# Tiles 3 and 7 by quarters in the second column half of the second products, their parts kept in idle buffers, two sums merged

## Chip, cores and metric

The kernel runs on one core of a Trainium2 chip. The metric is device time in microseconds: the median of three runs of the whole program. TensorE (PE) multiplies matrices, VectorE (DVE) and ScalarE (ACT) work element by element, GpSimd (POOL) does a few small steps, and SyncE (SP) issues most transfers. Each engine works through its own queue in order, and waits for the others by semaphores.

## The reference

A decoder layer over 512 tokens of 1024 columns: a SwiGLU feed-forward layer (FFN 1), a token mixer, and a second SwiGLU layer (FFN 2), all in float32, each between two RMS norms.

```python
def swiglu_ffn(x, w_in, w_out):
    gate, up = jnp.split(x @ w_in, 2, axis=-1)
    return (jax.nn.silu(gate) * up) @ w_out
...
x = x + 0.5 * rms_norm(swiglu_ffn(rms_norm(x, norm_pre[l, 0]), ffn1_w_in[l], ffn1_w_out[l]),
                       norm_post[l, 0])
mixed = token_mixer(rms_norm(x, norm_pre[l, 1]), w_mix_in[l], ...)
x = x + rms_norm(mixed, norm_post[l, 1])
x = x + 0.5 * rms_norm(swiglu_ffn(rms_norm(x, norm_pre[l, 2]), ffn2_w_in[l], ffn2_w_out[l]),
                       norm_post[l, 2])
```

D_MODEL is 1024, D_FF 2816, DEPTH 1. The change is in the second product of both feed-forward layers: h (512 x 2816) times w_out (2816 x 1024).

## The kernel before

Every float32 operand is kept as two parts, a rounded high part (a cast on ACT, line 273 for weights, 812 for h) and the remainder as a low part (a subtraction on DVE, line 275 for weights, 813 for h). A product of two such operands takes three matmuls: high by high, high by low, low by high.

`ffn_out` computes the second product. The 1024 output columns are done in two halves of 512. The 2816 rows of `w_out` are cut into 11 tiles of 256 rows; a tile's weights in one half are 256 x 512, held as 128 x 1024. `OUT[half]` gives the order of the tiles. Each tile is done in one of two ways:

- plain (line 893): 16 blocks of 128 x 128 by 256 columns, three matmuls each, 48 in all. DVE makes one low part of the weights (128 x 1024), and one of h, unless the tile's h is kept from the first half (`AGAIN`, tiles 9 and 10).
- by quarters (line 901), for the tiles in `QUARTERED[half]`: the Strassen-Winograd form with seven products of quarters instead of eight, 42 matmuls. It wants sums of quarters of the weights (`sum_quarters`, four operations 128 x 256 on DVE, line 306) and of h (`h_sums`, on DVE, line 844). Its weights come as two sets: first the low part of three quarters as loaded (128 x 768), then, once the sums stand and ACT has cast them, the low part of the four summed quarters (128 x 1024, the variable `v` in `quartered`). Between the last sum on DVE and the low part of `v` on DVE lies a cast on ACT.

The low and high parts of three quarters of h, the tile's "parts" (`h_quarters`), last from the first half to the second where both go by quarters, in places of the buffers of the transposed input (`x_place`, table `PLACES`; tiles 2, 4, 6, 8). Tiles 3 and 7, by quarters in the first half only, have their parts in two buffers of the "raw" ring for that time, and their sums in the scratch tile `hsum`. The summed h that `quartered` multiplies is split anew in each half, into a ring of three buffers (`s_place`).

`more` runs two or three tiles ahead of the products, so the order of the splits on ACT and DVE follows from `OUT`, `QUARTERED` and the depth of the rings. Weights are loaded into a ring of five buffers (raw2), and their split parts lie in four places (`WBUF`). A load is issued by SP when its buffer comes free; SP's queue is in order, and a load whose buffer isn't free holds what is behind it.

The last four tiles of the second half (`LAST = 4`) are done chunk by chunk: `chunk(i)` computes group i of 128 tokens over all four tiles, after which `post1` norms it and adds it to x, and after FFN 1 the mixer's norm, transposes and first products (`head`) follow. The common sums of the products by quarters (`common`, `add`, line 863) are added before chunk 0 is complete. In the first half of `ffn_out` all eleven tiles go through one after the other, and `post0` takes the half's result (y, line 475) from the PSUM banks while the second half begins.

Of the kernel before, what the change touches and what calls it, by code (L numbers as in the profile page):

```python
# [9 lines left out]
F32R = mybir.dt.float32r  # L10
AF = mybir.ActivationFunctionType
ALU = mybir.AluOpType
PSUM = bass.MemoryType.PSUM

P = 128
T = 512
D = 1024
# [5 lines left out]
RAW, WBUF, PAD, LATE, NEXT, FRONT, STEP = 3, 4, 128, 112, 64, 96, 16  # L23
PAIRS = NF // 2
# [54 lines left out]

QUARTERED = [(2, 3, 4, 6, 7, 8), (2, 4, 6, 8)]
OUT = [list(range(PAIRS)), [9, 2, 4, 10, 6, 8, 0, 1, 3, 5, 7]]
LAST = 4
PLACES, LATER = {2: 1, 4: 2, 6: 0, 8: 3}, {0: (1, 0), 7: (2, 3)}

AGAIN, ROWS = (9, 10), (18, 19, 20, 21)

# [27 lines left out]
class Layer:  # L116
# [705 lines left out]
    def h_quarters(self, k2, n=None):  # L822

        src = self.by_chunk(k2)
        parts = self.x_place(n) if n is not None else [
            self.wp.tile([P, D], F32R, tag="raw", bufs=RAW, name=self.nm("once"))[:, P - 2 * STEP :] for _ in range(2)
        ]
        parts = [v[:, : 3 * QUARTER].rearrange("p (k c t) -> p k c t", c=2, t=P) for v in parts]
        self.two_parts(*(v[:, 0] for v in parts), src[:, 0, 1])
        self.two_parts(*(v[:, 1:] for v in parts), src[:, 1])  # L830
        return [[None] + [v[:, j] for j in range(3)] for v in parts]
# [5 lines left out]
    def h_sums(self, k2, stay):  # L837

        a = self.by_chunk(k2)
        f = self.hf[:, 2 * k2 : 2 * k2 + 2, :]  # L840
        if not stay:
            f = self.sp.tile([P, 2, T], F32, tag="xn", bufs=1, name=self.nm("hsum"))
        v = f.rearrange("p k (c u t) -> p k u c t", u=2, t=P)
        tt = lambda out, x, y, op: self.nc.vector.tensor_tensor(out, x, y, op=op)
        tt(v[:, 0, 0], a[:, 0, 1], a[:, 0, 0], ALU.subtract)
        tt(v[:, 1, 0], v[:, 0, 0], a[:, 1, 0], ALU.add)
        for k in range(2):
            tt(v[:, k, 1], a[:, k, 1], v[:, 1, 0], ALU.subtract)
        return f

    def s_tile(self, f):
# [6 lines left out]
    def ffn_out(self, gpost_row, scale, after, trans, head):  # L858
# [4 lines left out]
        tt = lambda out, a, b, op: nc.vector.tensor_tensor(out, a, b, op=op)  # L863
        seq = [(half, k2) for half in range(2) for k2 in OUT[half]]
        made = deque((h, None) for h in self.hs)
# [3 lines left out]
        def more(n):  # L869
            while count[0] < min(n, len(seq)):  # L870
                half, k2 = seq[count[0]]
                count[0] += 1
                if k2 in QUARTERED[half]:
                    if k2 not in kept:
                        stay = k2 in QUARTERED[1]
                        kept[k2] = self.h_quarters(k2, PLACES.get(k2)), self.h_sums(k2, stay)
                    a, f = kept[k2]
                    made.append((a, self.s_tile(f)))
                elif half and k2 in AGAIN:
                    made.append(again.popleft())  # L880
                else:
                    made.append((self.h_tile(k2, self.x_place(*LATER[k2]) if half and k2 in LATER else None), None))
                    if not half and k2 in AGAIN:
                        again.append(made[-1])
# [47 lines left out]
        def add(C, T, u):  # L932
            for v in range(2):
                tt(C[u][v], C[u][v], T[u, v], ALU.add)
# [9 lines left out]
        for half in range(2):  # L944
            C = [[self.ps() for _ in range(2)] for _ in range(2)]
            M, T, left = None, None, len(QUARTERED[half])
            for m, k2 in enumerate(OUT[half][: PAIRS - LAST * half]):
                more(n + 2)
# [9 lines left out]
                else:  # L958
                    w = self.pull()
                    more(len(seq) if half and m == PAIRS - LAST - 1 else n + 3)  # L960
                    for i in (0, 2, 1, 3):
# [13 lines left out]
        ws = []  # L975
        for k2 in OUT[1][-LAST:]:
            ws.append(self.pull())
            more(n + 1)
            n += 1
        hs = [made.popleft()[0] for _ in range(LAST)]  # L980

        add(C, T, 1)

        def chunk(i):
            vn = [(v, n) for v in range(2) for n in range(LAST)]
            if i == 0:

                vn.sort(key=lambda f: f[1])
            for v, n in vn:
                plain(C, ws[n], hs[n], i, v, False)  # L990
                if v and i == NT - 1:
                    self.drop(ws[n])
                if v and n == LAST - 1 and i == 0:
                    add(C, T, 0)
                if n == LAST - 1:
                    yield 2 - v
# [78 lines left out]
    def ffn_items(self, name, w_in, w_out):  # L1075
# [47 lines left out]
        for h in range(2):  # L1123
            for k2 in OUT[h]:
                src = w_out[k2 * 2 * P : (k2 + 1) * 2 * P, h * 512 : (h + 1) * 512].rearrange("(k p) d -> p k d", p=P)
                key = (name, "out", h, k2)
                made.append(Item(key, [Load(key, src, 2, 512, "raw2", 5, 8)], sums=k2 in QUARTERED[h]))
                if k2 in QUARTERED[h]:
                    made.append(Item(key, ()))
# [688 lines left out]
```

## Time and profile before

| | |
|---|---|
| median of 3 runs | 937.53 us (937.38 to 937.99) |
| profiled execution | 939.23 us, span of the trace 937.5 us |
| PE busy | 929.0 us (99% of the span), 7471 matmuls and transposes |
| DVE busy | 772.9 us (82%) |
| ACT busy | 511.5 us (55%) |
| POOL busy | 107.1 us (11%) |

The second product of FFN 1 begins at about 224 us of the span and its last matmuls start at 340.79 us, with the mixer's first norm and transposes between them; that of FFN 2 begins at about 816 us and runs to the end. In rows of the timeline the columns are the start and the time until the last of the joined instructions ends (us), the engine, the line, the operation, what it writes and reads, shape and count; in brackets how long the engine stood idle before it and what released it. L275 is line 275.

### The profile page before, as it was taken

Reading aid. Unit: us, or ns where it says so; the run is one execution under the profiler, and the core shown is the slowest. Engines: PE = TensorE matmul, PEld = TensorE weight load, DVE = VectorE, ACT = ScalarE, POOL = GpSimd, SP = SyncE. Lnnn points to the kernel's source line nnn. Section 1 sums busy time; section 2 is a strip of 40 time slices with the busy share of each in tenths; the row PEclk is TensorE's granted clock in tenths of the full one; section 3 lists DMA queues with packets and bytes.
Section 4 is the critical chain, followed back from the end, with each engine's and each line's share of the span. In section 5 each row is a group of like instructions: output and inputs, shape, how many; then the busy total and the mean of one; then the engine's idle time right before and its main releaser. Section 6 shows DMA issues by size and latency. Waiting matters only on the chain.

```text
span 937.5 us, 18056 instructions
## 1 busy us (share of the span) xinstructions
PE 929.0 (99%) x7471; PEld 894.4 (95%) x7471; DVE 772.9 (82%) x1044; ACT 511.5 (55%) x735; POOL 107.1 (11%) x172
## 2 busy tenths in 40 slices
PE   9999999999999999999999999999999999999997
PEld 7999999999999999998887887899999999999997
DVE  6899988889988876698846665799899889998884
ACT  7645455557456467956632445595354545655541
POOL 3530000000001045200011310314000000000101
PEclk9999999999999999999999999999999999999999
DMA  9252443332352034421312124352354435324212
GB/s 317 89 157 91 128 126 108 99 108 78 116 164 91 24 87 121 111 68 45 91 45 68 46 91 143 104 181 67 115 158 135 136 116 157 108 90 131 78 45 91
DMA packets 86956, 101.35 MB, mean 108 GB/s; under 512 B 4277, under 2 KB 66777, under 8 KB 86874
## 3 DMA queue, kind: packets, MB, share of 16 engines
q1 hardware_dynamic: 86586, 99.68, 34.8%
q8 instruction: 58, 0.95, 0.4%
q10 hardware_dynamic: 288, 0.52, 0.2%
q14 instruction: 24, 0.20, 0.1%
HBM read 98.10 MB, written 2.10 MB: 107 GB/s over the span
## 4 chain that ended last, share of the span: by engine, by line
PE 61%; ACT 1%; DMA 0%; DVE 0%; issue 0%; POOL 0%; DVEq 0%; POOLq 0%; ACTq 0%; SPq 0%
PE ps L603 22%; PE ps L893 7%; PE ps L533 6%; PE ps L901 5%; PE ps L179 5%; PE ps L181 4%; PE ps L180 4%; PE ps L1307 2%; PE ps L348 1%; PE ps L543 1%; PE ps L1482 0%; DMA raw<-in_ffn_w_in_dram 0%; PE ps L1393 0%; PE ps L1589 0%; PE ps L1562 0%; PE ps L1348 0%
## 5 line engine op out<-in xcount | busy, mean ns | idle before, releaser
L273 ACT CAST w<-raw 128x1024 fp32r<-128x1024 f32 (+1 forms) x238 | 244.4, 1034 | 233.1 <-PE ps L603 93.5
L275 DVE TENSOR_TENSOR w<-raw,w 128x1024 fp32r<-128x1024 f32 (+1 forms) x238 | 291.6, 1232 | 36.1 <-ACT w L273 35.3
L603 PE MATMUL ps<-xq,w 128*128 128x256 f32 x2016 | 237.4, 277 | 0.0
L603 PEld LDWEIGHTS ps<-xq,w 128*128 128x128 f32 x2016 | 233.2, 188 | 0.0
L603 PE MATMUL ps<-sq,w 128*128 128x256 f32 x1512 | 178.3, 277 | 0.3
L603 PEld LDWEIGHTS ps<-sq,w 128*128 128x128 f32 x1512 | 174.6, 188 | 0.9 <-ACT ps L654 0.9
L893 PE MATMUL ps<-w,hs 128*128 128x256 f32 x960 | 113.0, 276 | 0.0
L893 PEld LDWEIGHTS ps<-w,hs 128*128 128x128 f32 x960 | 110.7, 188 | 0.0
L289 DVE TENSOR_TENSOR raw<-raw,raw 128x1024 f32<-128x1024 f32 x72 | 89.9, 1251 | 8.1 <-DMA raw<-in_ffn_w_in_dram 6.6
L179 PE MATMUL ps<-w,xq 128*128 128x512 f32 x192 | 78.8, 411 | 0.1
L180 PE MATMUL ps<-w,xq 128*128 128x512 f32 x192 | 74.9, 391 | 0.1
L181 PE MATMUL ps<-w,xq 128*128 128x512 f32 x192 | 75.0, 392 | 0.0
L438 POOL TENSOR_SCALAR col<-col 128x1 f32<-128x1 f32 x24 | 9.0, 377 | 513.8 <-ACT junk L437 513.7
L533 PE MATMUL ps<-xq,w 128*128 128x256 f32 x480 | 58.1, 282 | 0.0
L901 PE MATMUL ps<-w,hs 128*128 128x256 f32 x480 | 57.7, 276 | 0.0
L533 PEld LDWEIGHTS ps<-xq,w 128*128 128x128 f32 x480 | 56.9, 189 | 0.5 <-issue 0.5
L901 PEld LDWEIGHTS ps<-w,hs 128*128 128x128 f32 x480 | 55.9, 188 | 0.0
L179 PEld LDWEIGHTS ps<-w,xq 128*128 128x128 f32 x192 | 36.1, 188 | 8.3 <-issue 0.9
L181 PEld LDWEIGHTS ps<-w,xq 128*128 128x128 f32 x192 | 36.0, 188 | 8.2 <-DVE xq L355 0.3
L812 ACT CAST hs<-hf 128x1024 fp32r<-128x1024 f32 x32 | 33.7, 1052 | 17.4 <-PE ps L901 10.7
L180 PEld LDWEIGHTS ps<-w,xq 128*128 128x128 f32 x192 | 36.2, 188 | 7.2 <-DVE w L281 0.5
L813 DVE TENSOR_TENSOR hs<-hf,hs 128x1024 fp32r<-128x1024 f32 x32 | 39.1, 1221 | 1.3 <-ACT hs L812 1.2
(258 smaller groups left out, 1140.4 us busy)
## 6 DMA issues: line engine op xcount, KB each, us to landing
raw<-in_ffn_w_in_dram SPq DMA_DIRECT2D x98, 512.0 KB, 3.7
raw<-in_ffn_w_out_dram SPq DMA_DIRECT2D x44, 512.0 KB, 4.2
raw<-in_w_mix_in_dram SPq DMA_DIRECT2D x28, 512.0 KB, 3.7
raw<-in_w_mix_out_dram SPq DMA_DIRECT2D x8, 512.0 KB, 3.9
out_dram<-xs SPq DMA_DIRECT2D x8, 256.0 KB, 2.0
xs<-in_x_dram SPq DMA_DIRECT2D x6, 256.0 KB, 4.1
gpost<-in_norm_post_dram SPq DMA_DIRECT2D x3, 512.0 KB, 3.5
gpre<-in_norm_pre_dram SPq DMA_DIRECT2D x2, 512.0 KB, 4.5
```

Of the source, the lines that this page charges most:

```text
L179: mm(ps, sh, mh, start=start, stop=False, **kw)
L180: mm(ps, sh, ml, start=False, stop=False, **kw)
L181: mm(ps, sl, mh, start=False, stop=stop, **kw)
L273: nc.scalar.copy(hi, raw)
L275: self.low = nc.vector.tensor_tensor(lo, raw, hi.bitcast(F32), op=ALU.subtract)
L289: (nc.vector if late else nc.gpsimd).tensor_tensor(o, o, c, op=ALU.add)
L533: mm(ps[:, u0:u1], w[:, a, k, :], self.xop(k, b, u0, u1), start=k + n + m == 0, stop=k == ND - 1 and n == 2, skip_group_check=True,)
L603: self.nc.tensor.matmul(ps[:, c], wb[b][:, k, v], left[d][:, k, :], start=first and a + n + k == 0, stop=n == 2 and k == KH - 1, skip_grou ...
L812: self.nc.scalar.copy(hi, src)
L813: self.nc.vector.tensor_tensor(lo, src, hi.bitcast(F32), op=ALU.subtract)
L893: mm(out, a[kk][:, i * P : (i + 1) * P], w[:, b, kk, QUARTER * v : QUARTER * (v + 1)], start=begin and c == kk == n == 0, stop=kk == 1 and ...
L901: mm(ps[:, QUARTER * c : QUARTER * (c + 1)], A[a][:, c], B[b], start=begin and c == n == 0, stop=n == 2, skip_group_check=True,)
```

## The change

Tiles 3 and 7 go by quarters in the second half too, so both halves have the same six. Their parts now have to last into the second half: those of tile 3 stay in two buffers of "raw", those of tile 7 (`APART`) in one buffer of "raw" and in the tile of the norm's gain (`gpre`), which is not in use then. The sums of both stay in place in h (the `stay` branch of `h_sums`; the scratch `hsum` is no longer used). The second half's order is new, tile 10 moves from the fourth to the eighth place, and `LATER` names a place for tile 5's h alone. In `h_sums` two subtractions of 128 x 256 that share an operand become one of 128 x 512. The program has 7240 matmuls in its queue instead of 7264.

```diff
--- before.py
+++ after.py
@@ -79,10 +79,10 @@
 
 
 
-QUARTERED = [(2, 3, 4, 6, 7, 8), (2, 4, 6, 8)]
-OUT = [list(range(PAIRS)), [9, 2, 4, 10, 6, 8, 0, 1, 3, 5, 7]]
-LAST = 4
-PLACES, LATER = {2: 1, 4: 2, 6: 0, 8: 3}, {0: (1, 0), 7: (2, 3)}
+QUARTERED = [(2, 3, 4, 6, 7, 8), (2, 3, 4, 6, 7, 8)]
+OUT = [list(range(PAIRS)), [9, 2, 4, 3, 6, 8, 7, 10, 0, 1, 5]]
+LAST, APART = 4, 7
+PLACES, LATER = {2: 1, 4: 2, 6: 0, 8: 3}, {5: (2, 3)}
 
 AGAIN, ROWS = (9, 10), (18, 19, 20, 21)
 
@@ -822,9 +822,12 @@
     def h_quarters(self, k2, n=None):
 
         src = self.by_chunk(k2)
-        parts = self.x_place(n) if n is not None else [
-            self.wp.tile([P, D], F32R, tag="raw", bufs=RAW, name=self.nm("once"))[:, P - 2 * STEP :] for _ in range(2)
-        ]
+        once = lambda pool, tag, bufs, o: pool.tile([P, D], F32R, tag=tag, bufs=bufs, name=self.nm("once"))[:, o:]
+        if n is not None:
+            parts = self.x_place(n)
+        else:
+            places = [(self.wp, "raw", RAW, P - 2 * STEP), (self.cp, "gpre", 1, STEP // 2)]
+            parts = [once(*places[k2 == APART and m]) for m in range(2)]
         parts = [v[:, : 3 * QUARTER].rearrange("p (k c t) -> p k c t", c=2, t=P) for v in parts]
         self.two_parts(*(v[:, 0] for v in parts), src[:, 0, 1])
         self.two_parts(*(v[:, 1:] for v in parts), src[:, 1])
@@ -844,8 +847,7 @@
         tt = lambda out, x, y, op: self.nc.vector.tensor_tensor(out, x, y, op=op)
         tt(v[:, 0, 0], a[:, 0, 1], a[:, 0, 0], ALU.subtract)
         tt(v[:, 1, 0], v[:, 0, 0], a[:, 1, 0], ALU.add)
-        for k in range(2):
-            tt(v[:, k, 1], a[:, k, 1], v[:, 1, 0], ALU.subtract)
+        tt(v[:, :, 1], a[:, :, 1], v[:, 1:2, 0].broadcast_to([P, 2, 2, P]), ALU.subtract)
         return f
 
     def s_tile(self, f):
```

DVE's queue in the first half of FFN 1, from the low part of tile 6's first weights (raw2_159) to that of tile 7's summed weights (raw2_167), before; once_183 and once_184 are tile 7's parts, hsum_185 its sums, hs_186 its summed h, split:

```order
L275 TENSOR_TENSOR w_248<-raw2_159_2559,w_248 128x768
L813 TENSOR_TENSOR once_184_2950<-hf_2_83,once_183_2949 128x256
L306 TENSOR_TENSOR raw2_159_2559<-raw2_159_2559 128x256
L813 TENSOR_TENSOR once_184_2950<-hf_2_83,once_183_2949 128x512
L306 TENSOR_TENSOR raw2_159_2559<-raw2_159_2559 128x256 x3
L813 TENSOR_TENSOR hs_186_2960<-hsum_185_2955,hs_186_2960 128x1024
L275 TENSOR_TENSOR w_248<-raw2_159_2559,w_248 128x1024
L275 TENSOR_TENSOR w_248<-raw2_167_2663,w_248 128x768
L306 TENSOR_TENSOR raw2_167_2663<-raw2_167_2663 128x256 x4
L275 TENSOR_TENSOR w_248<-raw2_167_2663,w_248 128x1024
```

The same stretch after:

```order
L275 TENSOR_TENSOR w_248<-raw2_159_2559,w_248 128x768
L306 TENSOR_TENSOR raw2_159_2559<-raw2_159_2559 128x256 x4
L275 TENSOR_TENSOR w_248<-raw2_159_2559,w_248 128x1024
L275 TENSOR_TENSOR w_248<-raw2_167_2662,w_248 128x768
L813 TENSOR_TENSOR hs_184_2953<-hf_2_83,hs_184_2953 128x1024
L306 TENSOR_TENSOR raw2_167_2662<-raw2_167_2662 128x256 x4
L275 TENSOR_TENSOR w_248<-raw2_167_2662,w_248 128x1024
```

Tile 7's parts (two operations) and its summed h (now hs_184) no longer stand between the start of tile 6's weight sums and the low part of the summed weights (the 1024 that follows the sums): the parts are made earlier, among tile 2's weights, and the summed h stands behind tile 7's first weights. Nothing stands between a tile's last sum and its summed weights any more.

DVE's queue in the second half of FFN 1 where tiles 6 and 8 are made, before (raw2_192 is tile 6's weights, raw2_193 tile 8's):

```order
L275 TENSOR_TENSOR w_248<-raw2_192_3129,w_248 128x768
L306 TENSOR_TENSOR raw2_192_3129<-raw2_192_3129 128x256 x4
L275 TENSOR_TENSOR w_248<-raw2_192_3129,w_248 128x1024
L275 TENSOR_TENSOR w_248<-raw2_193_3151,w_248 128x768
L813 TENSOR_TENSOR hs_246_3534<-hf_2_83,hs_246_3534 128x1024
L306 TENSOR_TENSOR raw2_193_3151<-raw2_193_3151 128x256 x4
L275 TENSOR_TENSOR w_248<-raw2_193_3151,w_248 128x1024
```

After (raw2_190 is tile 6's weights, raw2_196 tile 8's, raw2_234 tile 7's; hs_243 and hs_245 are summed h):

```order
L275 TENSOR_TENSOR w_248<-raw2_190_3121,w_248 128x768
L306 TENSOR_TENSOR raw2_190_3121<-raw2_190_3121 128x256
L813 TENSOR_TENSOR hs_243_3522<-hf_2_83,hs_243_3522 128x1024
L306 TENSOR_TENSOR raw2_190_3121<-raw2_190_3121 128x256 x3
L275 TENSOR_TENSOR w_248<-raw2_196_3185,w_248 128x768
L275 TENSOR_TENSOR w_248<-raw2_190_3121,w_248 128x1024
L306 TENSOR_TENSOR raw2_196_3185<-raw2_196_3185 128x256
L813 TENSOR_TENSOR hs_245_3577<-hf_2_83,hs_245_3577 128x1024
L306 TENSOR_TENSOR raw2_196_3185<-raw2_196_3185 128x256 x3
L275 TENSOR_TENSOR w_248<-raw2_234_3358,w_248 128x768
L275 TENSOR_TENSOR w_248<-raw2_196_3185,w_248 128x1024
```

Here the first weights of the next tile (768) now stand between a tile's sums and its summed weights (1024), and tile 7 follows tile 8 with the same set of operations where before the plain tiles 0, 1, 3, 5 and 7 came.

## The prediction

> **What bounds the kernel now.** The page's first part and the waits of PE come first.
>
> ```profile
> PE 929.0 (99%) x7471; PEld 894.4 (95%) x7471; DVE 772.9 (82%) x1044; ACT 511.5 (55%) x735; POOL 107.1 (11%) x172
> ```
>
> ```profile
> PE ps L175 <- POOL ident masks.py:199: 1.5, 1, 1.5
> PE ps L603 <- ACT xq L368: 0.2, 1, 0.2
> ```
>
> PE is never idle for want of work, so matmuls taken out shorten the program, as long as whoever feeds PE keeps up. So I asked next how full the feeders are where the change works: the first and the second half of the columns of each second product (columns: window, its length, PE, PEld, DVE, ACT, POOL busy, clock, DMA).
>
> ```profile
> 224.00:282.47 58.47, 58.47 (x518) 58.47 (x517) 53.39 (x82) 29.39 (x37) 0.19 (x1) 1.00 0.43 128
> 282.47:323.27 40.80, 40.80 (x362) 40.80 (x361) 35.04 (x48) 22.88 (x35) 2.25 (x7) 1.00 0.20 64
> 815.84:874.31 58.47, 52.94 (x81) 1.00 0.36 110
> 874.31:915.11 40.80, 35.20 (x48) 1.00 0.20 63
> ```
>
> DVE is busy 53.4 of 58.5 us in a first half and 35.0 of 40.8 in a second half (the last two rows give DVE alone), ACT about half. PE has no gap, but DVE has only 5 to 6 us of air per half. PE's timeline gives the price of a tile, each row's start to the next tile's: by quarters 247.11 - 242.35 = 4.76 us (42 matmuls), plain 257.31 - 251.87 = 5.44 us (48), so 0.113 us a matmul at full clock.
>
> ```profile
> 242.35 1.52 PE L901 MATMUL ps<-w,once 128*128 128x256 f32 x12
> ...
> 247.11 1.52 PE L901 MATMUL ps<-w,xq 128*128 128x256 f32 x12
> ...
> 251.87 5.60 PE L893 MATMUL ps<-w,hs 128*128 128x256 f32 x48
> 257.31 1.52 PE L901 MATMUL ps<-w,xq 128*128 128x256 f32 x12
> ```
>
> **The matmuls.** Tiles 3 and 7 of the second halves go from 48 matmuls to 42: 2 x 6 per layer, 24 in all, 24 x 0.113 = 2.72 us less, or 1.36 us per feed-forward layer (FFN below). PE at 99% with LDWEIGHTS at 95% is the row for it. The Trainium skill (Perfetto Trace Analysis, Identifying the Most-Contended Engine) says that the engine with the highest occupancy is the one to lighten first; by that alone the sum would be -2.72 us. It is a rival below.
>
> **What a tile by quarters costs DVE.** DVE's timeline in the second half of before, first a stretch without waits:
>
> ```profile
> 284.20 0.95 DVE L275 TENSOR_TENSOR w<-raw,w 128x768 fp32r<-128x768 f32 x1
> 285.06 2.38 DVE L475 TENSOR_TENSOR y<-ps,gpost 128x256 f32<-128x256 f32 x6
> 287.36 1.80 DVE L306 TENSOR_TENSOR raw<-raw 128x256 f32<-128x256 f32 x4
> 289.20 1.23 DVE L813 TENSOR_TENSOR hs<-hf,hs 128x1024 fp32r<-128x1024 f32 x1
> ...
> 305.67 1.22 DVE L813 TENSOR_TENSOR hs<-hf,hs 128x1024 fp32r<-128x1024 f32 x1
> 306.81 1.22 DVE L275 TENSOR_TENSOR w<-raw,w 128x1024 fp32r<-128x1024 f32 x1
> ...
> 317.69 0.68 DVE L863 TENSOR_TENSOR hf<-ps,hf 128x512 f32<-128x512 f32 x1
> 318.29 1.29 DVE L863 TENSOR_TENSOR ps<-ps,hf 128x512 f32<-128x512 f32 x2
> ```
>
> Start to start: a split's low part costs 0.86 (768 wide) or 1.14 us (1024), four weight sums 1.8 (about 1.72 where something stands between them), a 512-wide operation 0.60, six y 2.3. A tile by quarters so asks of DVE 0.86 + 1.75 + 1.14 (summed weights) + 1.14 (summed h) = 4.9 us, more than the 4.76 that PE takes for it; a plain one 2.3 (or 1.14, where its h is kept) for 5.44. And there is a round trip: the summed weights' low part (v) needs ACT's cast, which needs the last sum.
>
> ```profile
> 295.41 1.80 DVE L306 TENSOR_TENSOR raw<-raw 128x256 f32<-128x256 f32 x4
> ```
>
> ```profile
> 297.30 1.78 ACT L273 CAST w<-raw 128x1024 fp32r<-128x1024 f32 x2 [2.37 <-DVE raw L306]
> ```
>
> ```profile
> 298.38 2.10 DVE L275 TENSOR_TENSOR w<-raw,w 128x1024 fp32r<-128x1024 f32 x2 [1.17 <-ACT w L273]
> ```
>
> Sums end at 297.21, v begins at 298.38: 1.18 us, idle unless the queue has something in between.
>
> **First half, walked along the new queue.** Its work changes little, its order does (the two pieces of DVE's first half above): tile 7's parts and the sums of tile 3 no longer stand between a tile's weight sums and its v. The waits of before:
>
> ```profile
> 225.19 0.96 DVE L275 TENSOR_TENSOR w<-raw,w 128x768 fp32r<-128x768 f32 x1
> 226.06 0.43 DVE L844 TENSOR_TENSOR hf<-hf 128x256 f32<-128x256 f32 x1
> 226.39 0.43 DVE L306 TENSOR_TENSOR raw<-raw 128x256 f32<-128x256 f32 x1
> ...
> 230.72 1.23 DVE L275 TENSOR_TENSOR w<-raw,w 128x1024 fp32r<-128x1024 f32 x1 [0.74 <-ACT w L273]
> ...
> 259.05 1.23 DVE L275 TENSOR_TENSOR w<-raw,w 128x1024 fp32r<-128x1024 f32 x1 [1.17 <-ACT w L273]
> ...
> 266.32 2.36 DVE L275 TENSOR_TENSOR w<-raw,w 128x1024 fp32r<-128x1024 f32 x2 [1.19 <-ACT w L273]
> ```
>
> From tile 2's weights (225.1) in the new order: 0.86, three merged sums 1.8, four weight sums and two short h sums at 0.335 each 2.0, summed h 1.14, tile 7's parts 0.94: v of 2 begins near 231.9. Ten operations further (8.2, and 0.3 of waits) v of 3 at 240.4. Then, with a bare 1.18 each time: v of 4 after 1.14 + 1.14 + 0.98 + 1.26 + 1.14 + 0.42 + 1.18 = 7.26, at 247.7; v of 6 after 7.4 at 255.05; v of 7 after 6.1 at 261.15; v of 8 after 7.26 at 268.4, where before has 266.32. It ends at 269.6. PE wants it at 224.0 + 5.44 + 2.72 (p4) + 5.44 + 3 x 4.76 + 5.44 + 2 x 4.76 + 2.04 (18 matmuls of 8) + 0.11 = 269.0: a stall of 0.7 us where before had 1.4 to spare. The merge gives 2 x 0.335 - 0.60 = 0.07 us each: small, and already in the walk; a 512-wide sum with a repeated operand isn't in the trace, and between no saving (0.67) and that of a copy of half the reads (0.4) it is 0.2 us either way per layer. FFN 2 comes to its place earlier, 0.72 us after its half's start (815.84) instead of 1.19, and walks the same with 0.56 us in hand: stall 0.1.
>
> ```profile
> 816.56 0.96 DVE L275 TENSOR_TENSOR w<-raw,w 128x768 fp32r<-128x768 f32 x1
> ```
>
> **Second half.** From v of 8 on the queue is that of before, 2.0 us late, so tile 4's weights (284.20) begin at 286.2: 3.0 us after PE's half starts (282.47 + 0.7), not 1.7. From there to the last weights, those of tile 5, the new queue holds five 768s 4.3, six y 2.3, twenty sums 8.6, seventeen 1024s (five summed h, five v, four plain weights, three h) 19.3, two of the common sums 1.2, and waits for ACT of 2.0 (1.18 for 3; 0.3, 0.4, 0.1 for 6, 8, 7, where the next tile's 768 fills in: the two pieces of the second half): 37.8 us with the last one's tail, to t = 40.85. PE wants it in chunk 0 after 5.44 + 6 x 4.76 + 3 x 1.36 + 0.11 = 38.2. So PE loses 2.7 in the run of six tiles and gains 1.36: chunk 0 ends at 42.15 instead of 40.80. Net of the layer: FFN 1 +0.7 + 1.35 = +2.0, FFN 2 +0.1 + 1.35 = +1.5. Before had room here:
>
> ```profile
> 319.48 1.22 DVE L275 TENSOR_TENSOR w<-raw,w 128x1024 fp32r<-128x1024 f32 x1
> 322.79 1.38 DVE L863 TENSOR_TENSOR ps<-ps,hf 128x512 f32<-128x512 f32 x2 [2.10 <-PE ps L893]
> ```
>
> **What follows FFN 1.** The sums into C at 322.79 wait for PE now; after, they stand behind DVE's queue: last weights begin at t = 39.6, then 1.14 and four 0.60: 43.2, against 40.3; with 0.7 that is 3.5 us later. On them hangs, link by link (ACT square, POOL power, DVE x, norm, transposes), the first weight of the mixer:
>
> ```profile
> 339.67 1.07 ACT L354 CAST xq<-ps 128x512 fp32r<-128x512 f32 x2
> 340.61 1.07 ACT L273 CAST w<-raw 128x1024 fp32r<-128x1024 f32 x1
> ```
>
> ```profile
> 341.74 6.13 PE L543 MATMUL ps<-xq,w 128*128 128x256 f32 x48
> ```
>
> PE's start at 341.74 is the end of that cast (341.68), so here FFN 1 costs the chain's 3.5, not 2.0; the least is 2.0, if the chain has air. In FFN 2 it has:
>
> ```profile
> 921.18 0.42 DVE L485 TENSOR_TENSOR hf<-ps,gpost 128x256 f32<-128x256 f32 x1 [1.89 <-ACT junk L437]
> ```
>
> **The rest.** The load of gpre, now behind a mixer weight that waits for tile 7's end (about 318.7), lands 4.5 us (below) to 9 us later, its first reader stands at 329.4 + 3.5: nothing. Without that cover it would cost its 4.5. The mixer's first weights wait for tile 3's places (free near 303) and are read at 341 or later: nothing. Tile 5's output weights stand on SP's queue behind one of them, and issue before tile 8's split frees their place anyway.
>
> ```profile
> gpre<-in_norm_pre_dram SPq DMA_DIRECT2D x2, 512.0 KB, 4.5
> ```
>
> Sum: +3.5 + 1.5 = +5.0 us. The profiled execution took 939.23 us (span 937.5), 1.7 more than the median 937.53; it would take 944.2, the median 942.5. An error of 0.5 us in a layer's queue counts twice: 940.5 to 945.2.
>
> **Rivals.** (1) Only second halves are late: DVE makes up its bubbles in the first halves, and tile 4's weights begin at t = 1.7. Then the queue ends at 39.56, chunk 0 loses 0.06, the chain of FFN 1 1.56, FFN 2 gains 0.1: 939.0. For it, DVE has 5 us of air there; against it, the air is the bubbles themselves. Chance 0.13. (2) The gain lands, the rule above: DVE ends its queue of a second half by t = 38.2, 2.7 us sooner than I walk it. PE then keeps its 24 matmuls: 934.8. It needs both halves' waits for ACT (2.0 and 2.0) filled, which the order as it stands doesn't show. Chance 0.09. (3) Worse: PE's stalls free weight places later, ACT casts later, and DVE waits again; half a round trip in each of four late tiles per layer, 4 x 0.6 x 2 = 4.8: 947. Chance 0.09. The order has 24 matmuls fewer, so that part does what it says.
>
> **How the numbers follow.** The forecast keeps 0.69. Low 938.8 takes in rival 1 but not rival 2, high 945.2 the queue's error but not rival 3. A difference under 0.2% (1.9 us) can't be told from none. Faster is rival 2, 0.09; same most of rival 1, 0.09; slower the rest, 0.82.
>
> **What would show it.** PE waits for DVE w L275 in the second products, 0 before, 5 us after; DVE's waits in the first half 5.9 instead of 4.3; the second halves near 42 us, not 40.8; PE idle 1.5 us at the mixer's start. It is wrong if PE stays gapless in both layers, or v of 8 begins before 267.5 in FFN 1.

## The result, and the profile after

The changed kernel took 945.28 us (median of 5 runs, 944.16 to 945.94) against 937.53 us for the kernel before on the same chip (5 runs, 937.12 to 938.7): 1.0080 times as long, with a 95% interval of 1.0068 to 1.0091. A second group of runs (e10 below) gave 943.12 against 937.40, 1.0066 (1.0049 to 1.0083). It is slower by 5.7 to 7.8 us. The profiled execution took 945.94 us, its span is 944.1 us, 6.6 more than before's 937.5.

The page of the changed kernel, first part: 24 matmuls fewer, DVE 8 us busier.

```profile
PE 930.5 (99%) x7447; PEld 893.3 (95%) x7447; DVE 781.2 (83%) x1052; ACT 512.4 (54%) x739; POOL 106.0 (11%) x172
```

PE's waits, changed kernel (line, releaser, us in total, times, longest). Before had only the second and the sixth row. Of the new ones the last lies in FFN 2's first product; all the others are in or right behind the second products, and DVE ends all of these but the mixer's (L543).

```profile
PE ps L903 <- DVE w L275: 2.2, 4, 0.7
PE ps L175 <- POOL ident masks.py:199: 1.5, 1, 1.5
PE ps L543 <- ACT w L273: 1.4, 1, 1.4
PE ps L895 <- DVE hs L813: 0.8, 2, 0.4
PE ps L895 <- DVE w L275: 0.4, 2, 0.2
PE ps L603 <- ACT xq L368: 0.2, 1, 0.2
PE ps L603 <- ACT w L273: 0.2, 1, 0.2
```

The stages are measured between rows of PE's timeline. In the kernel before, the second products begin here:

```profile
223.99 5.60 PE L893 MATMUL ps<-w,hs 128*128 128x256 f32 x48
...
815.67 5.60 PE L893 MATMUL ps<-w,hs 128*128 128x256 f32 x48
```

In the changed kernel: the two starts, the first half's stall, the run of six tiles by quarters in the second half (289.35 to 319.58) with its stall, the wait in chunk 0, the end of chunk 0 (the start of chunk 1, 326.22), and the mixer's first product.

```profile
224.43 5.60 PE L895 MATMUL ps<-w,hs 128*128 128x256 f32 x48
...
268.63 0.96 PE L903 MATMUL ps<-w,hs 128*128 128x256 f32 x7
270.30 2.21 PE L903 MATMUL ps<-w,hs 128*128 128x256 f32 x17 [0.71 <-DVE w L275]
...
273.03 16.48 PE L895 MATMUL ps<-w,hs 128*128 128x256 f32 x144
289.35 1.52 PE L903 MATMUL ps<-w,xq 128*128 128x256 f32 x12
...
306.65 2.21 PE L903 MATMUL ps<-w,hs 128*128 128x256 f32 x17 [0.71 <-DVE w L275]
...
310.74 3.19 PE L903 MATMUL ps<-w,hs 128*128 128x256 f32 x24
...
319.58 3.11 PE L895 MATMUL ps<-w,hs 128*128 128x256 f32 x26
323.11 1.42 PE L895 MATMUL ps<-w,hs 128*128 128x256 f32 x10 [0.42 <-DVE hs L813]
...
326.22 2.20 PE L895 MATMUL ps<-w,hs 128*128 128x256 f32 x18
...
345.94 0.39 PE L543 MATMUL ps<-xq,w 128*128 128x256 f32 x1 [1.35 <-ACT w L273]
...
820.44 5.60 PE L895 MATMUL ps<-w,hs 128*128 128x256 f32 x48
```

The second half starts two plain tiles (10.88 us) behind the row of 144 matmuls. Stage by stage, in us:

| | before | changed | difference |
|---|---|---|---|
| start-up and first product, to FFN 1's second product | 223.99 | 224.43 | +0.44 |
| FFN 1, first half | 58.48 | 59.48 | +1.00 |
| FFN 1, second half to the end of chunk 0 | 40.80 | 42.31 | +1.51 |
| end of chunk 0 to the mixer's first product | 18.47 | 19.72 | +1.25 |
| mixer and FFN 2's first product | 473.93 | 474.50 | +0.57 |
| FFN 2, first half | 58.48 | 59.10 | +0.62 |
| FFN 2, second half to the end of chunk 0 | 40.80 | 42.05 | +1.25 |
| end of chunk 0 to the end | 22.55 | 22.51 | -0.04 |

The second product of FFN 1 with what hangs on it lost 3.76 us, that of FFN 2 1.83, together 5.59. The 1.0 us outside of them lies in stages whose instructions the change leaves alone.

The view of waits shows only a part of this. At their own pace of 0.1133 us the matmuls of the second products need 58.48 and 39.44 us (348 matmuls) a layer; in the changed kernel the four halves took 7.1 us more than that (1.00 + 2.87 + 0.62 + 2.61), while the waits listed for them add up to 3.4. Two parts of the rest can be read off the rows: short stops that a joined row hides (the 24 matmuls at 310.74 take 3.19 us, elsewhere 2.88) and slower matmuls right behind a stop: the 17 from 270.30 took 2.05 us to the next row (272.35), 0.12 more than 17 x 0.1133. The table goes by starts, so it has all of it.

The two halves, FFN 1 and then FFN 2, changed kernel (columns: window, its length, PE, PEld, DVE, ACT, POOL busy, granted clock, DMA):

```profile
224.43:283.91 59.48, 58.77 (x519) 58.57 (x518) 52.65 (x77) 27.86 (x33) 0.00 (x0) 1.00 0.31 98
283.91:326.22 42.31, 40.88 (x351) 39.90 (x349) 39.51 (x59) 24.77 (x39) 2.45 (x8) 1.00 0.38 113
820.44:879.54 59.10, 58.77 (x519) 58.57 (x517) 52.31 (x76) 27.95 (x33) 0.00 (x0) 1.00 0.36 108
879.54:921.59 42.05, 40.89 (x351) 39.90 (x350) 39.53 (x59) 24.91 (x39) 2.44 (x8) 1.00 0.20 63
```

In a second half DVE is now busy for 39.5 us, where PE alone would be through in 48 + 6 x 42 + 48 = 348 matmuls, 39.4 us. DVE's timeline in the first half: the bare waits at the summed weights of tiles 4, 6, 7 and 8, as walked.

```profile
248.21 2.36 DVE L275 TENSOR_TENSOR w<-raw,w 128x1024 fp32r<-128x1024 f32 x2 [1.19 <-ACT w L273]
...
255.61 2.09 DVE L275 TENSOR_TENSOR w<-raw,w 128x1024 fp32r<-128x1024 f32 x2 [1.20 <-ACT w L273]
...
261.75 1.23 DVE L275 TENSOR_TENSOR w<-raw,w 128x1024 fp32r<-128x1024 f32 x1 [1.20 <-ACT w L273]
...
269.02 2.36 DVE L275 TENSOR_TENSOR w<-raw,w 128x1024 fp32r<-128x1024 f32 x2 [1.19 <-ACT w L273]
```

And in the second half: one tile by quarters takes DVE from 305.37 to 310.43, 5.06 us with a wait of 0.25 in it; the last weights begin at 323.58; the additions to chunk 0 are the second and third of the last row.

```profile
305.37 1.23 DVE L275 TENSOR_TENSOR w<-raw,w 128x1024 fp32r<-128x1024 f32 x1 [0.25 <-ACT w L273]
...
310.43 1.22 DVE L275 TENSOR_TENSOR w<-raw,w 128x1024 fp32r<-128x1024 f32 x1 [0.25 <-ACT w L273]
...
323.58 1.21 DVE L275 TENSOR_TENSOR w<-raw,w 128x1024 fp32r<-128x1024 f32 x1
...
326.51 1.88 DVE L865 TENSOR_TENSOR ps<-ps,hf 128x512 f32<-128x512 f32 x3
```

### The profile page after: what moved, and what is told of

Same layout as the page of the kernel before. It is cut to its first block, busy times and chain, and to the rows that moved or that the text cites. A ratio compares the mean times of both kernels' runs of the same rounds, so it can differ in the third digit from the quotient of the medians.

```text
span 944.1 us, 18026 instructions
## 1 busy us (share of the span) xinstructions
PE 930.5 (99%) x7447; PEld 893.3 (95%) x7447; DVE 781.2 (83%) x1052; ACT 512.4 (54%) x739; POOL 106.0 (11%) x172
## 4 chain that ended last, share of the span: by engine, by line
PE 52%; DVE 7%; ACT 2%; issue 2%; DMA 0%; POOL 0%; DVEq 0%; POOLq 0%; ACTq 0%; SPq 0%
PE ps L603 22%; PE ps L533 6%; PE ps L179 5%; PE ps L181 4%; PE ps L180 4%; PE ps L895 3%; DVE w L275 2%; PE ps L1309 2%; DVE raw L306 2%; DVE hs L813 2%; ACT w L273 1%; PE ps L348 1%; PE ps L543 1%; PE ps L1484 0%; DMA raw<-in_ffn_w_in_dram 0%
## 5 line engine op out<-in xcount | busy, mean ns | idle before, releaser
L273 ACT CAST w<-raw 128x1024 fp32r<-128x1024 f32 (+1 forms) x242 | 247.3, 1031 | 251.5 <-PE ps L603 89.9
L275 DVE TENSOR_TENSOR w<-raw,w 128x1024 fp32r<-128x1024 f32 (+1 forms) x242 | 295.0, 1225 | 38.1 <-ACT w L273 37.1
L895 PE MATMUL ps<-w,hs 128*128 128x256 f32 x864 | 102.3, 277 | 0.8 <-DVE hs L813 0.8
L903 PE MATMUL ps<-w,hs 128*128 128x256 f32 x576 | 71.5, 278 | 2.4 <-DVE w L275 2.2
L533 PE MATMUL ps<-xq,w 128*128 128x256 f32 x480 | 58.1, 282 | 0.0
L533 PEld LDWEIGHTS ps<-xq,w 128*128 128x128 f32 x480 | 56.9, 189 | 0.5 <-issue 0.5
L813 DVE TENSOR_TENSOR hs<-hf,hs 128x1024 fp32r<-128x1024 f32 x38 | 46.2, 1216 | 0.0
L812 ACT CAST hs<-hf 128x1024 fp32r<-128x1024 f32 x38 | 39.8, 1049 | 4.3 <-DVE hf L847 3.6
```

The lines of the kernel that those rows point to most:

```text
L273: nc.scalar.copy(hi, raw)
L275: self.low = nc.vector.tensor_tensor(lo, raw, hi.bitcast(F32), op=ALU.subtract)
L533: mm(ps[:, u0:u1], w[:, a, k, :], self.xop(k, b, u0, u1), start=k + n + m == 0, stop=k == ND - 1 and n == 2, skip_group_check=True,)
L812: self.nc.scalar.copy(hi, src)
L813: self.nc.vector.tensor_tensor(lo, src, hi.bitcast(F32), op=ALU.subtract)
L895: mm(out, a[kk][:, i * P : (i + 1) * P], w[:, b, kk, QUARTER * v : QUARTER * (v + 1)], start=begin and c == kk == n == 0, stop=kk == 1 and ...
```

## The experiments

The order of a queue is chosen by a scheduler that works with its own estimates, so most edits move some neighbours too; what each did is read from its trace. All stand in one table: from the start of FFN 1's second product to the mixer's first product, from the start of FFN 2's to the end of the span (both from the profile's PE rows, as above), the sum against before's 239.58, and the medians with the ratio to the kernel before in the same group.

| run | FFN 1 | FFN 2 | sum, against before | median, before in the group | ratio (95%) |
|---|---|---|---|---|---|
| before | 117.75 | 121.83 | | | |
| changed | 121.51 | 123.66 | +5.59 | 945.28, 937.53 | 1.0080 (1.0068 to 1.0091) |
| e1 | 119.07 | 122.25 | +1.74 | 939.06, 937.52 | 1.0015 (1.0006 to 1.0024) |
| e2 | 118.73 | 122.47 | +1.62 | 939.36, 937.52 | 1.0027 (1.0016 to 1.0038) |
| e3 | 122.99 | 123.36 | +6.77 | 945.11, 937.52 | 1.0081 (1.0066 to 1.0096) |
| e4 | 121.04 | 122.36 | +3.82 | 942.51, 937.52 | 1.0052 (1.0035 to 1.0069) |
| e5 | 119.28 | 122.25 | +1.95 | 940.25, 937.74 | 1.0029 (1.0018 to 1.0040) |
| e6 | 117.72 | 121.84 | -0.02 | 937.84, 937.74 | 0.9999 (0.9990 to 1.0007) |
| e7 | 118.91 | 122.66 | +1.99 | 940.49, 937.74 | 1.0034 (1.0021 to 1.0046) |
| e8 | 120.37 | 123.99 | +4.78 | 942.32, 937.74 | 1.0054 (1.0040 to 1.0068) |
| e9 | 119.24 | 120.63 | +0.29 | 939.28, 937.40 | 1.0019 (1.0009 to 1.0029) |
| e10 | 121.59 | 123.66 | +5.67 | 943.12, 937.40 | 1.0066 (1.0049 to 1.0083) |
| e11 | 119.95 | 121.82 | +2.19 | 940.84, 937.40 | 1.0036 (1.0023 to 1.0049) |
| e12 | 117.74 | 120.47 | -1.37 | 936.41, 937.67 | 0.9984 (0.9975 to 0.9993) |

**e1: the second halves without the weights' sums.**

```diff
-            self.sum_quarters(self.quarters(self.raw[it.key]))
+            if it.key[2] == 0:
+                self.sum_quarters(self.quarters(self.raw[it.key]))
```

> The changed kernel, but the sums of the weights' quarters are left out in both second halves of the columns (6 tiles x 4 operations of 0.335 us a layer, about 8 us of DVE's queue and the round trip over ACT), so the output is not the reference's. Theory (DVE's queue sets the second halves): PE then runs a second half at its own pace, 39.4 us from its start to the end of chunk 0 where the changed kernel took 42.3 and 42.05; the mixer's head comes another 1.25 us sooner; the first halves' stalls (1.0 and 0.6) stay. 945.3 - 2.9 - 2.6 - 1.25 = 938.5. Rival (the new order, the new places or ACT's casts make the loss, not the amount of DVE's work): second halves stay near 42, time 943 or more.

The six tiles by quarters now run without a gap: in PE's timeline from 289.33 to 317.89, 28.56 us, which is 6 x 4.76.

```profile
289.33 1.52 PE L904 MATMUL ps<-w,xq 128*128 128x256 f32 x12
...
317.89 4.47 PE L896 MATMUL ps<-w,hs 128*128 128x256 f32 x38
322.56 1.21 PE L896 MATMUL ps<-w,hs 128*128 128x256 f32 x8 [0.21 <-DVE hs L814]
```

The time is 939.06, the theory's 938.5 within 0.6, far from the rival's 943. New places and loads and the order of the tiles are as in the changed kernel, so they are not what costs. The edit takes the sums' work and the round trip over ACT away together; it does not tell the two apart (e5 does). What remains over before is the first halves' stalls and a new, small wait in chunk 0 for a low part of h.

**e2: the changed first halves, the old second halves.**

```diff
-QUARTERED = [(2, 3, 4, 6, 7, 8), (2, 3, 4, 6, 7, 8)]
-OUT = [list(range(PAIRS)), [9, 2, 4, 3, 6, 8, 7, 10, 0, 1, 5]]
+QUARTERED = [(2, 3, 4, 6, 7, 8), (2, 4, 6, 8)]
+OUT = [list(range(PAIRS)), [9, 2, 4, 10, 6, 8, 0, 1, 3, 5, 7]]
...
-PLACES, LATER = {2: 1, 4: 2, 6: 0, 8: 3}, {5: (2, 3)}
+PLACES, LATER = {2: 1, 4: 2, 6: 0, 8: 3}, {0: (1, 0), 7: (2, 3)}
...
-                        stay = k2 in QUARTERED[1]
+                        stay = True
```

> The first halves as in the changed kernel (parts of tiles 3 and 7 in the new places, sums in place, same order on DVE up to the second half), the second halves with the order and the four tiles by quarters of before. Tiles 3 and 7 then multiply their summed h in the second half, so the output is not the reference's. Theory: the first halves keep their stalls (1.0 and 0.6 us before tile 8's summed weights), and the second halves, whose queue on DVE had 2.1 us to spare, take 40.8 as before: 937.5 + 1.6 = 939.1. Rival 1 (the first half's new order is harmless): 937.5. Rival 2 (a late start costs the second half as much again): 941.

Both layers keep the first halves' stalls (+0.98 and +0.64) and no more: second halves of 40.80, as before. So the loss splits: 1.6 us from the first halves' new order, 4.0 (5.6 - 1.6) from the second halves and what hangs on them. Both rivals of this run fall.

**e3 and e4: the products y taken off DVE where it is late.**

```diff
-            self.nc.vector.tensor_tensor(y[:, v], ps, g[:, v], op=ALU.mult)
+            if scale == 1.0:
+                self.nc.vector.tensor_tensor(y[:, v], ps, g[:, v], op=ALU.mult)
+            else:
+                self.nc.scalar.copy(y[:, v], ps)
...
-            nc.vector.tensor_tensor(o, ps, g[:, 512 + v.start : 512 + v.stop], op=ALU.mult)
+            last = nc.vector.tensor_tensor(o, ps, g[:, 512 + v.start : 512 + v.stop], op=ALU.mult)
+        if out is not None:
+            with self.behind(last):
+                nc.vector.tensor_tensor(y, y, g[:, :512], op=ALU.mult)
```

> The changed kernel with the eight products y = ps x gpost a layer taken off DVE at the start of the second half: ACT copies ps to y (8 x 0.38 us), and DVE multiplies y by the gain in the chunk stage, where it waits for POOL 0.64 us. DVE's queue of a second half is 2.7 us shorter. Theory: second halves at about 39.5 us, the mixer's head 1.25 sooner, first halves' stalls stay: 945.3 - 2.8 - 2.6 - 1 = 939 to 940. Rival 1 (not the amount of DVE's work): 945. Rival 2 (ACT's copies, 3 us, delay its casts and DVE's summed weights with them): 942 to 944.

> The same edit of y in the kernel before. Theory: PE never waits there, so 2.7 us less in DVE's queue gives nothing: 937.5, at most 0.6 more where the product of y lies on the chain to the mixer's head. Rival (any relief of DVE helps, since it is at 82%): 934 to 936.

Both theories missed; e3's 945.11 is the time that its rival 1 gave. In e4, where PE had no wait, the edit alone cost 5.0 us, 3.8 of them in the two stages of the table and 1.2 outside, unexplained: the product of y went onto the chain from chunk to chunk, and PE waited 2.9 us for the mixer's first weight.

```profile
345.81 4.45 PE L549 MATMUL ps<-xq,w 128*128 128x256 f32 x23 [2.91 <-ACT w L273]
```

In e3 the second half gained only 0.9 (42.31 to 41.38). ACT's queue, first two rows, had the eight copies between its squares, its cast of the next h ended at 290.93, and DVE, third row, waited 1.98 us for it: what DVE's queue lost came back as a wait for ACT.

```profile
289.54 0.43 ACT L478 COPY y<-ps 128x256 f32<-128x256 f32 x1
289.79 1.14 ACT L818 CAST hs<-hf 128x1024 fp32r<-128x1024 f32 x1
```

```profile
290.96 1.22 DVE L819 TENSOR_TENSOR hs<-hf,hs 128x1024 fp32r<-128x1024 f32 x1 [1.98 <-ACT hs L818]
```

From that row to the start of the last weights DVE's queue took 31.5 us (322.49 - 290.96), and 31.6 in the changed kernel (323.58 - 292.00): the same queue, a little earlier. As a test of the amount of DVE's work this says nothing, for or against, since the edit costs more elsewhere than it could bring.

**e5 and e6: the low part of h put into the gaps.** No operation is added or taken away, only the order on DVE is.

```diff
-            self.nc.vector.tensor_tensor(b[out], b[a], b[c], op=ALU.add)
+            self.summed = [self.nc.vector.tensor_tensor(b[out], b[a], b[c], op=ALU.add)]
...
-        self.nc.vector.tensor_tensor(lo, src, hi.bitcast(F32), op=ALU.subtract)
+        with self.behind(*after):
+            self.nc.vector.tensor_tensor(lo, src, hi.bitcast(F32), op=ALU.subtract)
```

Here `after` is `self.summed` for h tiles and summed h, and empty for the parts.

> The changed kernel with one rule more for the order: the low part of h (1.14 us on DVE) is issued behind the last sum of the weights issued so far, so that it stands in the 1.18 us in which DVE waits for ACT's cast of the summed weights; no instruction is added or left out. Theory (the loss is DVE's queue, its waits for ACT included): the first halves' stalls go (1.0 and 0.6), DVE's queue of a second half has 35.8 us of work from 1.7 us on and is done by 37.5, before PE wants its last weights at 38.2, so PE runs without gaps and keeps its 24 matmuls: 937.5 - 2.7 = 934.8, at most 937. Rival 1 (the amount of DVE's work is too much in any order): second halves near 41, 938 to 940. Rival 2 (not DVE's queue): 945.

> The same rule for the order in the kernel before, where PE never waits. Theory: 937.5, no difference. Rival (the rule helps by itself, through the stages after the second halves): 936 or less.

In the changed kernel the rule took back 3.6 of the 5.6 us, in the kernel before nothing. The first halves are 58.48 in both layers, no stall; the six tiles of the second halves run without a gap. What is left is one wait of 1.50 us in each layer's chunk 0, for the last low part of h. PE, and DVE where that low part (321.70) stands behind the common sums of L866:

```profile
322.97 1.20 PE L896 MATMUL ps<-w,hs 128*128 128x256 f32 x8 [1.50 <-DVE hs L814]
```

```profile
318.17 0.68 DVE L866 TENSOR_TENSOR hf<-ps,hf 128x512 f32<-128x512 f32 x1
318.77 0.69 DVE L866 TENSOR_TENSOR ps<-ps,hf 128x512 f32<-128x512 f32 x1
319.37 0.68 DVE L866 TENSOR_TENSOR hf<-ps,hf 128x512 f32<-128x512 f32 x1
319.97 1.21 DVE L275 TENSOR_TENSOR w<-raw,w 128x1024 fp32r<-128x1024 f32 x1
321.10 0.68 DVE L866 TENSOR_TENSOR hf<-hf,ps 128x512 f32<-128x512 f32 x1
321.70 1.21 DVE L814 TENSOR_TENSOR hs<-hf,hs 128x1024 fp32r<-128x1024 f32 x1
```

So the theory's 937 at most was missed, and 940.25 is near the time that rival 1 gave (938 to 940), though by one misplaced operation and not by the amount of work alone: e9 moves it, and PE's gaps are gone.

**e7: PE's work taken away.**

```diff
-                for n, (a, b) in enumerate(((0, 0), (0, 1), (1, 0))):
+                for n, (a, b) in enumerate(((0, 0), (0, 1), (1, 0))[: 3 - half]):
```

> The changed kernel with the third matmul of each product (low part of h by high part of the weights) left out in the tiles by quarters of the second halves: 6 x 14 x 0.113 = 9.5 us less of PE's work a layer, the splits and sums as they are, so the output is a little off. Theory (DVE sets the second halves): the end of chunk 0 moves by no more than the 2 to 3 us that DVE still waits there: 942 to 945. Rival (PE's own pace or its weight loads set them): 945.3 - 19 = 926.

PE has 19 us less to do; the time fell by 2.6 us against e10 (940.49, 943.12) and by 4.8 against the first measurement. Its second half of FFN 1 begins at 284.45, 48 matmuls before the tile that starts at 290.10 (they start 0.1178 us apart here). In it DVE is busy 38.74 of 40.03 us (columns as above):

```profile
284.45:324.48 40.03, 34.59 (x266) 33.00 (x265) 38.74 (x59) 25.02 (x39) 2.45 (x8) 0.96 0.31 93
```

That is 97%, against 86% for PE, and the rival's 926 is far off: the second halves are DVE's. The time is 1.5 below the theory's range. The trace shows one reason: the scheduler changed DVE's order here too and filled its waits for ACT in this half (0.55 us are left of 1.67).

**e8: the two sums apart again.**

```diff
-        tt(v[:, :, 1], a[:, :, 1], v[:, 1:2, 0].broadcast_to([P, 2, 2, P]), ALU.subtract)
+        for k in range(2):
+            tt(v[:, k, 1], a[:, k, 1], v[:, 1, 0], ALU.subtract)
```

> The changed kernel with the two sums of h apart again (two operations of 128 x 256 for one of 128 x 512, six times a layer). By the traces 2 x 0.335 against 0.60: 0.07 us each, 0.4 a layer where DVE is late. Theory: 945.3 to 946. Rival (the operand repeated by a stride of zero costs DVE or delays what follows): 944.5 or less.

942.32, 0.8 below e10 in the median and 0.9 in the stages: on the rival's side of the expectation. It does not settle what the merge is worth: the scheduler ordered DVE's first half differently, and tile 8's summed weights began 43.67 us after the start in FFN 1 (268.14 - 224.47) where the changed kernel has 44.59 (269.02 - 224.43). FFN 1's first half got 0.85 shorter by that. In FFN 2 the same weights came 0.27 later than in the changed kernel (860.99 - 816.51 = 44.48 against 864.65 - 820.44 = 44.21), and behind the stall there PE ran 4% slower besides (see the last section), so FFN 2's 123.99 mixes two things. DVE's row in FFN 1:

```profile
268.14 2.36 DVE L275 TENSOR_TENSOR w<-raw,w 128x1024 fp32r<-128x1024 f32 x2 [1.19 <-ACT w L273]
```

The merged operation itself takes 0.60 to 0.61 us, start to start, where two apart took 0.67; the order that came with it weighs more: 0.92 us earlier in FFN 1, 0.27 later in FFN 2.

**e9, e10 and e11: the common sums last.** e9 is e5 with these lines; e11 has the same order in the kernel before; e10 is the changed kernel again.

```diff
-                    if left == 0:
+                    if left == 0 and half == 0:
...
-        add(C, T, 1)
+        with self.behind(*self.split_h[-3:], self.low):
+            T = common(M, [self.hf[:, j, :] for j in ROWS])
...
                 if v and n == LAST - 1 and i == 0:
                     add(C, T, 0)
+                if v and n == LAST - 1 and i == 1:
+                    with self.behind(self.weighed):
+                        add(C, T, 1)
```

`split_h` holds the low parts of h, `low` the last low part of the weights, `weighed` the last product by the gain of chunk 0.

> The kernel of e5 with the common sums of the second half (four operations of 512 columns that wait for nothing else) and the two additions to the odd chunks put behind the last low parts of h and of the weights, since e5's PE lost 1.5 us a layer waiting for the last low part of h, which stood behind such sums. Theory (every loss is the order of DVE's queue): PE runs both halves without gaps, 58.5 and 39.4 us; DVE ends the additions to chunk 0 near 324.1 for a start at 224.5, 0.6 sooner than before. From the start of the second product to the mixer's first product 117.1 us (117.75 before, 121.5 changed), from the start of FFN 2's to the end 120.5 (121.8 before, 123.7 changed): 937.6 - 2.0 = 935.6. Rival (the buffers of h, freed by PE itself, or the amount of DVE's work hold it still): as e5, 938 to 940.

> The changed kernel once more, unedited, on the chip and beside the runs of before that the other kernels of this group share. Theory: 117.75 + 3.8 and 121.8 + 1.8 us for the two second products and what hangs on them, 5.6 in all: 943 to 944. Rival (the 7.75 us between the medians have a cause outside of the two second products): 945.3 again, with the rest lost in between.

> The same order of DVE's queue in the kernel before (four tiles by quarters in the second halves). Theory: PE has no gaps to close there, 937.6, at most 0.6 more for the additions to chunk 1 that stand later. Rival (the order helps by itself, and e9's gain is not the 24 matmuls): as e9.

In e9 PE runs both halves of both layers without a gap, 58.48 and 39.44 us: the 24 matmuls are kept, 1.36 us a layer. PE's rows of chunk 0, chunk 1 and the mixer:

```profile
317.23 4.24 PE L896 MATMUL ps<-w,hs 128*128 128x256 f32 x36
...
322.67 2.20 PE L896 MATMUL ps<-w,hs 128*128 128x256 f32 x18
...
343.99 6.12 PE L543 MATMUL ps<-xq,w 128*128 128x256 f32 x48 [2.01 <-ACT w L273]
```

FFN 2 takes 120.63, as expected. But the theory's 935.6 was missed by 3.7: FFN 1's head takes the gain back, 21.32 us from the end of chunk 0 (322.67) to the mixer, 18.47 before. By the stages e9 is 0.3 above before, by the medians 1.9; its profiled execution (938.23) was faster than its median, and the rest of that difference is not explained. The additions to chunk 1, L866 below, came later than expected: the first only at 327.75, when PE was through with most of chunk 1, the second behind the norm (L465), and the later chunks queue behind it.

```profile
327.75 0.69 DVE L866 TENSOR_TENSOR ps<-ps,hf 128x512 f32<-128x512 f32 x1
329.91 1.42 DVE L465 SCALAR_TENSOR_TENSOR xn<-xs,col,gpre 128x512 f32<-128x512 f32 x2 [1.46 <-POOL col L442]
331.25 0.69 DVE L866 TENSOR_TENSOR ps<-ps,hf 128x512 f32<-128x512 f32 x1
```

e11 shows that this placing is what costs: without any tile more by quarters it made FFN 1's stage 2.2 us longer, where 0.6 at most was expected, and FFN 2's not at all. e10 repeated the changed kernel's stages to 0.1 us (+5.67), and its median, 5.7 above before, agrees with them.

**e12: FFN 1 as before, FFN 2 as in e9.** The tables by layer; which functions read which is left out.

```diff
+QUARTERED1, QUARTERED2 = ([(2, 3, 4, 6, 7, 8), t] for t in ((2, 4, 6, 8), (2, 3, 4, 6, 7, 8)))
+OUT1 = [list(range(PAIRS)), [9, 2, 4, 10, 6, 8, 0, 1, 3, 5, 7]]
+OUT2 = [list(range(PAIRS)), [9, 2, 4, 3, 6, 8, 7, 10, 0, 1, 5]]
```

> FFN 1 word for word as before (four tiles by quarters in its second half, the order of before); FFN 2 with the change and with the order of e9. In e9 FFN 1's second product lost to its tail what PE gained, but FFN 2's took 120.6 us from its start to the end, against 121.8 before. Theory (where nothing hangs on DVE's additions the 12 matmuls are kept): FFN 1 117.75, FFN 2 120.6 us: 1.2 less than before, 936.2 to 936.5. Rival (the gain of e9's FFN 2 came from its earlier start or from the state it was entered in): 121.8 in FFN 2, 937.5.

936.41 us, as expected, 0.9984 times the kernel before (0.9975 to 0.9993): a version faster than both, if by only 0.16% over the kernel before. Chunk 0 of FFN 2 runs from 906.91 to 912.36, 97.93 us after that product's start at 814.43, where before took 99.28.

```profile
814.43 5.60 PE L903 MATMUL ps<-w,hs 128*128 128x256 f32 x48
...
906.91 4.24 PE L903 MATMUL ps<-w,hs 128*128 128x256 f32 x36
...
912.36 2.20 PE L903 MATMUL ps<-w,hs 128*128 128x256 f32 x18
```

## Why the prediction was right

The mechanism was the one forecast: DVE's queue, not PE, sets the second products once six tiles go by quarters in both halves. e1, e5 and e7 show it three ways: less work for DVE, a better order of the same work, and less work for PE. The signs named beforehand came, one of them smaller: the second halves took 42.31 and 42.05 us (near 42 forecast), DVE's waits for ACT in FFN 1's first half were 5.98 us (5.9), PE was idle 1.35 us at the mixer's start (1.5), but PE's listed waits for the weights' low parts (DVE w L275) add up to 2.6 us and not 5, for the reason given under the table of stages. Step by step:

- **Matmuls.** 24 fewer, as counted; e9 and e12 show the price of 1.36 us a layer. Rival 2 would have given 934.8; the changed kernel's trace disagrees. The Trainium skill's next section (Perfetto Trace Analysis, Optimization Strategy) says that the most-contended engine can change over time. In the changed kernel the shares alone do not show such a change, not even in the second half of FFN 1: PE is still counted busy 97% (40.88 of 42.31 us), its weight loads 94%, DVE 93% (39.51). Only in e7 does DVE lead, 97% against 86%. What told the two apart was a price per tile on each engine, 5.06 us on DVE against 4.76 on PE.
- **Price of a tile on DVE.** Forecast 4.9 us and 0.1 to 0.4 of waiting on top; measured 5.06, 0.25 of it waiting.
- **First half.** Bare waits of 1.18 at tiles 4, 6, 7 and 8: measured 1.19 to 1.20. Tile 8's summed weights 44.4 us after the start (268.4 - 223.99): measured 44.59. The stall in FFN 1 was 1.0, not 0.7; in FFN 2 it was 0.62, not 0.1. That second term was mis-sized, in part by a misreading: the prediction takes 815.84 for FFN 2's start, but PE's row has it at 815.67. So DVE came to tile 2's weights 0.89 us after the start already in the kernel before (816.56 - 815.67), not 0.72, and again 0.89 in the changed one (821.33 - 820.44), where FFN 1 has 1.13 (225.56 - 224.43): FFN 2's lead was 0.24 and not 0.47 us, let alone the 0.56 of the walk.
- **Second half.** 1.35 a layer forecast; 1.51 and 1.25 measured. The prediction put the whole loss of 2.7 us into the run of six tiles. In FFN 1 that run lost 1.67 us (30.23, 289.35 to 319.58, where 6 x 4.76 is 28.56), and chunk 0 lost 1.20 more (6.64, 319.58 to 326.22, where 48 matmuls take 5.44), on the last low part of h and the last weights. The last weights begin 39.67 us after the half's start (323.58 - 283.91), forecast 39.6.
- **Chain to the mixer.** FFN 1 in all +3.5 forecast, +3.76 measured. The additions to chunk 0 begin 43.2 us after the half's start (326.51 + 0.60 - 283.91), as walked.
- **FFN 2's tail.** Air enough, as said: 22.51 against 22.55.
- **gpre and the mixer's weights.** The trace shows no wait for gpre in the mixer's norm. ACT waits 0.74 us for one mixer weight, 0.79 before. POOL's new wait of 3.34 us on such a load did not come again in e10.
- **Sum.** +5.0 forecast for the profile, +5.6 in the two stages (5.59 and 5.67) and +6.6 over the spans. The median of the first group, 945.28, lies 0.08 above the range's top; that of the second, 943.12, is inside. The first group's extra 2 us are not explained: 1.0 of the profiled execution lie in stages whose instructions the change leaves alone (0.44 at the start-up, 0.57 between the mixer and FFN 2, with a wait of 0.23 for ACT among them), and e10, the same kernel, did not have them.

Rival 1 (DVE makes its bubbles good) fell with the changed kernel's trace and with e2: the first halves did stall. Rival 2's condition, that DVE's waits for ACT be filled, was named rightly: e5 fills them, the stalls of the tiles go, and e9 keeps all 24 matmuls. What the prediction did not see is that the last h and the common sums would then be next: that is one misplaced operation, 1.5 us a layer. Rival 3 put 4.8 us of further waits on top; the second halves came out within 0.2 us of the walk without them.

## What to carry to other kernels

Before matmuls are saved by preparing operands on another engine, price a tile on that engine in the stage where it happens, start to start, with its round trips; a mean share of 82% can hide a stage at 93%, and even there PE's share was the higher one. A gap of about one round trip in an in-order queue is the place for an operation that nothing waits for yet: filling such gaps with work that was there anyway returned 3.6 of 5.6 us here. And try the halves of a change apart: with the order of e9 the same edit was a loss in FFN 1 (119.24 against 117.75 us), where the mixer's head hangs on DVE's last additions, and a gain in FFN 2 (120.63 against 121.83), where nothing does.

## What was not expected of the hardware

The same 288 matmuls of the mixer (L533; the line number differs with the edits) took 34.09 us in the first profiles of both kernels and 32.80 us in every later profile, by the timeline, with a mean granted clock of 0.999 in the first and 0.996 to 0.999 in the others. The same step of 4% stands within one execution: the 144 plain matmuls at the end of a first half take 16.48 us everywhere but in e7, where they take 17.12 in both layers, and in e8's FFN 2:

```profile
865.08 17.12 PE L896 MATMUL ps<-w,hs 128*128 128x256 f32 x144
```

They start 0.1178 us apart there instead of 0.1133, while the windows from 862 to 920 us give a granted clock of 1.00. In e8 the slower pace begins with the matmuls behind the stall before 862.27 and ends with those behind a wait at 916.55. What sets it stays open. It touches both first profiles alike and cancels between these two; whether the other executions of the first group had it is not recorded, so it may be a part of that group's unexplained 2 us.
